# Down product of a gated FFN on one Trainium2 core: a Strassen recurrence with sums in SBUF, replaced by a plain product summed in PSUM over split operands that are prepared pair by pair

## Chip, cores and metric

One NeuronCore of a Trainium2 chip runs the whole kernel. The metric is the device time of one execution in microseconds (us); lower is better. TensorE (PE), VectorE (DVE), ScalarE (ACT), GpSimd (POOL) and the DMA queue of SyncE (SP) run side by side, each in its own instruction order, and wait for one another through semaphores.

## The reference

Two decoder layers over 1024 positions of width 1024, in float32. Layer 0 mixes with a recurrent mixer (RWKV-7), layer 1 with sparse attention (DSA); each mixer is followed by the same gated FFN. The change lies in the last lines of that FFN, in both layers:

```python
def conv_ffn(x, w_up, conv_w, conv_b, w_down):
    u = x @ w_up                                  # (1024, 1024) @ (1024, 5632)
    u = causal depthwise convolution of u, width 3, + conv_b
    gate, val = jnp.split(u, 2, axis=-1)
    return (jax.nn.silu(gate) * val) @ w_down     # (1024, 2816) @ (2816, 1024)
...
x = layer_norm(DN_ALPHA * x + f, ln_g[i, 1], ln_b[i, 1])
```

## The kernel before

`trunk` chains four phases: `rwkv`, `ffn` of layer 0, `dsa`, `ffn` of layer 1. Each is a generator, and `drive` lets a phase begin while the one ahead of it finishes: every `yield` of the phase ahead gives one turn to the next. A float32 product is made from two rounded parts: `split` (L54, L60) rounds an operand into a high part on ACT (L54) and subtracts it on POOL or DVE to get the low part (L60), and `mm3` (L65, L66, L67) issues three matmuls, high by high, high by low and low by high. What order the instructions of an engine stand in is decided when the program is built; within an engine nothing overtakes.

The FFN first makes the gated hidden rows and stores them to DRAM as eleven pairs of 128 rows, `hd[0]` to `hd[10]` (`gated`, L1039 to L1049). This part, the up product, is the same before and after. The down product then multiplies these 2816 rows with `w_down`.

Before, the down product is a Strassen-Winograd product: a pair p gives a 2 by 2 scheme of 512-wide blocks (two row blocks of the contraction; two halves of the positions, two halves of the columns), and seven products (`11`, `12`, `S1`, `S2`, `S3`, `S4`, `22`) take the place of eight. `d_load` reads a pair's hidden rows and weight rows, 1 MB each (L1135, L1136). `d_op` makes the sums and differences on DVE (`sub`, L908, and L1147) and splits the result (L54 on ACT, L60 on POOL or DVE). `down` runs the matmuls of one product for one block of 128 positions over the pairs of a group, into a PSUM bank (`dn`), and `add_to` adds that bank to the running sum `acc` in SBUF on DVE (L1166) before the next step may use the bank. Groups hold two or three pairs (`cuts`): ten pairs in layer 0, nine in layer 1. The blocks left over (`tail`: two in layer 0, four in layer 1) are multiplied plainly at the end (`dt`, L1260), row block by row block, each followed by the LayerNorm of these 128 positions and the store (`norm_store`, L149; the steps of the norm are L92 to L111).

In layer 0 this end is interleaved with the start of `dsa`, which loads `uq` and `uk`, multiplies them (`wqk`, L1326) in two groups with one load of `uk` each, splits and stores the results (L1334), loads and splits eight `win` tiles (L1339), then reads back the normed rows (`xr`, L1310), transposes them (`pt`, L1357) and starts the `win` product. All these DMAs go through SP's one queue, in order.

Of the kernel before, what the change touches and what calls it, by code (L numbers as in the profile page):

```python
# [7 lines left out]
F32 = mybir.dt.float32  # L8
F32R = mybir.dt.float32r
# [5 lines left out]
D = 1024  # L15
# [868 lines left out]
def ffn(k, layer, src, dst):  # L884
# [120 lines left out]
    def bank(name, pool=None):  # L1005
        return (pool or PX).tile([128, 512], F32, name=name, tag="b", bufs=4)
# [117 lines left out]
    NPAIR = NF // 2
    cuts = [0, 3, 6, 8, 10] if layer == 0 else [0, 3, 6, 9]
    groups = [range(a, b) for a, b in zip(cuts, cuts[1:])]
    in_P = (0, 3, 4, 8, 9) if layer == 0 else (0, 3, 6, 8)
    tail = range(2 * cuts[-1], NF)
    acc = []
    R = {}  # L1130

    def d_load(p):
        r = R[p] = dict(raw=big("raw", P_ if p in in_P else L_, (128, 8, 512), F32))
        raw = r["raw"]
        nc.sync.dma_start(raw[:, 0:4].rearrange("p (f a) c -> p f (a c)", f=2), hd[p].rearrange("f p c -> p f c"))  # L1135
        nc.sync.dma_start(  # L1136
            raw[:, 4:8].rearrange("p (f a) c -> p f (a c)", f=2),
            k.w_down[layer, p * 256 : (p + 1) * 256, :].rearrange("(f p) c -> p f c", p=128),
        )

    def d_op(p, n, pool, lo_eng):

        r = R[p]
        raw = r["raw"]
        if n == "S1":
            q = r["q"] = sm("q")
            nc.vector.tensor_tensor(q[:, 0], raw[:, 1], raw[:, 3], ALU.add)  # L1147
            sub(q[:, 1], raw[:, 5], raw[:, 4])
        elif n == "S2":
            q = r["q"]  # L1150
            sub(q[:, 0], q[:, 0], raw[:, 0])
            sub(q[:, 1], raw[:, 7], q[:, 1])
        elif n == "S3":
            sub(raw[:, 1:6:4], raw[:, 0:8:7], raw[:, 1:6:4])
        elif n == "S4":
            sub(raw[:, 2], raw[:, 2], r["q"][:, 0])
        elif n == "22":
            sub(raw[:, 6], raw[:, 6], r["q"][:, 1])
        hi, lo = t4("dh", F32R, pool, (128, 2, 512)), t4("dl", F32R, pool, (128, 2, 512))
        r[n] = hi, lo  # L1160
        at = {"11": slice(0, 5, 4), "12": slice(2, 7, 4), "S3": slice(1, 6, 4), "S4": slice(2, 8, 5), "22": slice(3, 7, 3)}
        split(k, raw[:, at[n]] if n in at else r["q"], hi, lo, "a", lo_eng)

    def add_to(hf, tt, ch, ps, first):
        o = acc[hf][:, tt, 512 * ch : 512 * ch + 512]
        nc.vector.scalar_tensor_tensor(o, o, ALPHA if first else 1.0, ps, ALU.mult, ALU.add)  # L1166

    B_ = {}

    def down(gi, n, tt):  # L1170
        new = n in ("11", "12", "S1")
        x = n in ("11", "S2", "S3", "22")
        if new:
            B_[x, tt] = bank("dn", PX if x else PY)
# [11 lines left out]
    for p in groups[0]:
        d_load(p)
    for hf in range(2):
        a = big("acc", L_, (128, 4, 1024), F32)
        acc.append(a)  # L1190
        for tt in range(4):
            nc.sync.dma_start(a[:, tt], src[(4 * hf + tt) * 128 : (4 * hf + tt + 1) * 128, :])
    ng = len(groups)
    dsteps = [(gi, n) for gi in range(ng) for n in ("11", "12", "S1", "S2", "S3", "S4", "22")]
    done = set()

    def d_ops(j):
        if j < len(dsteps) and j not in done:
            done.add(j)
            gi, n = dsteps[j]  # L1200
            for i, p in enumerate(groups[gi]):
                d_op(p, n, N_ if i == 2 else P_, CFG["dl0"][3 * j + i] if j < 3 else "v" if i == 2 and n in ("11", "12", "S4") else "p")

    hs = []

    def tail_op(f):

        if layer == 1 and f == NF - 1:
            room = [t4("to", F32R, N_) for _ in range(4)]
        else:  # L1210
            room = big("to", L_, (128, 4, 1024))
            room = [room[:, i] for i in range(4)]
        for i, ap in enumerate((hd[f // 2][f % 2], k.w_down[layer, f * 128 : (f + 1) * 128, :])):
            raw = t4("tr")
            nc.sync.dma_start(raw, ap)
            split(k, raw, room[2 * i], room[2 * i + 1], "a", "p")
        hs.append(room)

    late = [NF - CFG["gl"] + i for i in range(CFG["gl"])]
    for j, (gi, n) in enumerate(dsteps):  # L1220
        for x in CFG["ga"] if j == 0 else "":
            if x == "g":
                gated(late.pop(0))
            else:
                d_ops(int(x))
        d_ops(j)
        if n == "11" and gi + 1 < ng:
            for p in groups[gi + 1]:
                d_load(p)
        d_ops(j + 1)  # L1230
        if j == 0:
            while late:
                gated(late.pop(0))
        if gi == ng - 1 and n in ("S2", "S3", "S4") and (i := ("S2", "S3", "S4").index(n)) < len(tail):
            tail_op(tail[i])
        for tt in range(4):
            down(gi, n, tt)
    if len(tail) > 3:
        tail_op(tail[3])
    lnw = []  # L1240
    for z in range(2):
        if layer == 0:
            lnw.append(L_.tile([128, D], F32, name=f"lnw{z}"))
        else:
            lnw.append(sm("lnw").rearrange("p a b -> p (a b)"))
        i = B_LN + 4 * layer + 2 + z
        nc.sync.dma_start(lnw[z], k.bvec[i : i + 1, :].to_broadcast([128, D]))
# [3 lines left out]
    for tt in range(8):
        tsl = slice(128 * tt, 128 * tt + 128)
        r = [acc[tt // 4][:, tt % 4, 512 * ch : 512 * ch + 512] for ch in range(2)]
        sums = L_.tile([128, 2], F32, name="lns", tag="lns", bufs=2)
        for ch in range(2):
            cs = slice(512 * ch, 512 * ch + 512)
            ps = bank("dt")
            for i, (a, b, c, d) in enumerate(hs):
                mm3(k, ps, (a[:, tsl], b[:, tsl]), (c[:, cs], d[:, cs]), i == 0, i == len(hs) - 1)
            nc.vector.scalar_tensor_tensor(  # L1260
                r[ch], r[ch], 1.0, ps, ALU.mult, ALU.add, accum_out=sums[:, ch : ch + 1]
            )
        kw = {} if layer else dict(sums=sums, junk=L_.tile([128, 512], BF16, name="lnj", tag="lnj", bufs=1))
        norm_store(k, L_, r, lnw, dst, 128 * tt, CFG["ln4"][layer] if tt < 7 else "pv", **kw)
# [711 lines left out]
```

## Time and profile before

| what | value |
|---|---|
| time, median of 3 runs | 3173.01 us (3172.37 to 3178.31) |
| the profiled execution | 3170.01 us |
| its span in the profile | 3168.0 us |
| mean granted TensorE clock | 0.937 of full speed |
| PE busy | 2834.0 us (89%) |
| DVE busy | 2463.5 us (78%) |
| POOL busy | 1528.7 us (48%) |
| ACT busy | 1368.9 us (43%) |

The busy shares are means over four phases with different limits, so the stage in question is read by itself: a table of stages first (busy time of each engine and the granted clock in a stretch), then the waits ahead of the matmuls of that stretch, then the time line of the engine that is waited for. The granted clock is given as a share of 2.4 GHz; its two levels are 1.00 and 0.50.

### The profile page before, as it was taken

What the parts mean: (1) busy time and instruction counts of PE and PEld (TensorE: products, weight loads), DVE (VectorE), ACT (ScalarE), POOL (GpSimd) and SP (SyncE); (2) the same over time, 40 slices, a digit from 0 to 9 for tenths busy, and PEclk for the clock granted to TensorE, in tenths of its full rate; (3) what the DMA queues carried; (4) which work ended last, traced back from release to release, by engine and by line L of the source; (5) the groups of instructions that cost most, each with busy time, mean ns of one, the idle gap of its engine ahead of it and who ended that gap; (6) DMA issues with size and microseconds to landing.
All of it is one profiled execution on the core that took longest, in us unless ns stands there. A gap on an engine that the chain in (4) does not pass through costs nothing. (4 is left out here: it accounts for less than half of the span.)

```text
span 3168.0 us, 41686 instructions
## 1 busy us (share of the span) xinstructions
PE 2834.0 (89%) x15032; PEld 2217.4 (70%) x15032; DVE 2463.5 (78%) x3911; ACT 1368.9 (43%) x2353; POOL 1528.7 (48%) x987
## 2 busy tenths in 40 slices
PE   7789998898988999997888888889998899998798
PEld 3577576786866777775667765667776677777577
DVE  6776776768576888889786699995675888888965
ACT  4433243322233544443224487784363444444231
POOL 3525045140246666666677222212214666666766
PEclk9889998898998999998998989899999999999899
DMA  6645435344162222244115221113224222225212
GB/s 214 246 152 195 142 121 199 134 148 146 64 201 89 80 80 80 80 143 189 41 40 173 102 90 37 34 40 115 77 66 151 60 80 80 80 81 206 80 53 93
DMA packets 235232, 354.87 MB, mean 112 GB/s; under 512 B 17194, under 2 KB 110762, under 8 KB 234642
## 3 DMA queue, kind: packets, MB, share of 16 engines
q1 hardware_dynamic: 221202, 327.04, 31.6%
q10 hardware_dynamic: 13824, 25.17, 2.2%
q8 instruction: 118, 1.93, 0.3%
q14 instruction: 88, 0.72, 0.1%
HBM read 248.99 MB, written 103.15 MB: 111 GB/s over the span
## 5 line engine op out<-in xcount | busy, mean ns | idle before, releaser
L60 POOL TENSOR_TENSOR wo<-wr,wo 128x512 fp32r<-128x512 f32 x220 | 414.3, 1907 | 289.4 <-ACT wo L54 289.4
L1039 DVE SCALAR_TENSOR_TENSOR cv<-u,vec,cv 128x1023 f32<-128x1023 f32 (+1 forms) x176 | 348.0, 1995 | 52.9 <-ACT cv L1034 51.2
L65 PE MATMUL dn<-dh 128*128 128x512 f32 x532 | 220.3, 414 | 67.8 <-DVE acc L1166 67.8
L60 POOL TENSOR_TENSOR dl<-raw,dh 128x1024 fp32r<-128x1024 f32 x82 | 220.2, 2708 | 102.2 <-ACT dh L54 96.7
L65 PE MATMUL p<-xT,wo 128*128 128x512 f32 x528 | 213.1, 404 | 27.8 <-ACT u L1023 18.2
L66 PE MATMUL dn<-dl,dh 128*128 128x512 f32 x532 | 218.1, 410 | 14.3 <-DVE dl L60 7.5
L1671 POOL TENSOR_TENSOR cm<-sc,toep 128x256 f32<-128x256 f32 x96 | 75.7, 795 | 298.1 <-DVE mn L1687 229.7
L1034 ACT ACTIVATE cv<-u,vec 128x1024 f32<-128x1024 f32 x88 | 109.5, 1244 | 250.2 <-DVE u L1028 249.6
L67 PE MATMUL dn<-dh,dl 128*128 128x512 f32 x532 | 217.0, 408 | 0.0
L67 PE MATMUL p<-xT,wo 128*128 128x512 f32 x528 | 208.8, 395 | 2.9 <-POOL wo L60 2.9
L66 PE MATMUL p<-xT,wo 128*128 128x512 f32 x528 | 208.5, 395 | 3.0 <-DVE xT L60 3.0
L1166 DVE SCALAR_TENSOR_TENSOR acc<-acc,dn 128x512 f32<-128x512 f32 x196 | 131.0, 680 | 86.3 <-PE dn L67 86.3
L60 POOL TENSOR_TENSOR wo<-S,wo 128x512 fp32r<-128x512 f32 x88 | 173.3, 1987 | 30.0 <-ACT wo L54 25.7
L54 ACT CAST dh<-raw 128x1024 fp32r<-128x1024 f32 x95 | 94.8, 1047 | 199.6 <-issue 81.1
L65 PEld LDWEIGHTS dn<-dh 128*128 128x128 f32 x532 | 106.3, 200 | 98.5 <-DVE acc L1166 42.2
L60 POOL TENSOR_TENSOR wl<-wr,wh 128x512 fp32r<-128x512 f32 x56 | 76.3, 1363 | 181.7 <-ACT wh L54 109.1
L65 PEld LDWEIGHTS p<-xT,wo 128*128 128x128 f32 x528 | 100.7, 191 | 65.4 <-ACT u L1023 33.0
L65 PE MATMUL p<-x,wo 128*128 128x512 f32 x352 | 138.9, 394 | 3.4 <-DVE x L60 3.0
L54 ACT CAST wo<-wr 128x512 fp32r<-128x512 f32 x220 | 127.2, 619 | 27.3 <-POOL wo L60 18.6
L67 PE MATMUL p<-x,wo 128*128 128x512 f32 x352 | 138.4, 393 | 0.0
L66 PE MATMUL p<-x,wo 128*128 128x512 f32 x352 | 138.4, 393 | 0.0
L66 PEld LDWEIGHTS dn<-dl,dh 128*128 128x128 f32 x532 | 106.5, 200 | 38.4 <-DVE dl L60 8.4
(412 smaller groups left out, 8552.0 us busy)
## 6 DMA issues: line engine op xcount, KB each, us to landing
wr<-in_w_up_dram SPq DMA_DIRECT2D x88, 512.0 KB, 5.9
hd<-cv SPq DMA_DIRECT2D x44, 512.0 KB, 3.4
raw<-hd SPq DMA_DIRECT2D x19, 1024.0 KB, 5.0
raw<-in_w_down_dram SPq DMA_DIRECT2D x19, 1024.0 KB, 7.6
wr<-in_w_wo_dram SPq DMA_DIRECT2D x68, 256.0 KB, 2.9
wr<-in_w_rkv_dram SPq DMA_DIRECT2D x48, 256.0 KB, 4.3
kept_w<-wh ACTq DMA_DIRECT2D x48, 256.0 KB, 3.5
kept_w<-wl SPq DMA_DIRECT2D x48, 256.0 KB, 3.0
```

Source lines behind the costliest of these rows:

```text
L54: nc.scalar.copy(hi, raw)
L60: eng.tensor_tensor(lo, raw, f32(hi), ALU.subtract)
L65: mm(ps, lhs[0], rhs[0], start=start, stop=False, **kw)
L66: mm(ps, lhs[0], rhs[1], start=False, stop=False, **kw)
L67: mm(ps, lhs[1], rhs[0], start=False, stop=stop, **kw)
L1034: nc.scalar.activation(o, u, AF.Identity, bias=k.vec[:, cb : cb + 1], scale=k.vec[:, cw[2] : cw[2] + 1])
L1039: nc.vector.scalar_tensor_tensor(o[:, d:], u[:, : 1024 - d], k.vec[:, cw[j] : cw[j] + 1], o[:, d:], ALU.mult, ALU.add)
L1166: nc.vector.scalar_tensor_tensor(o, o, ALPHA if first else 1.0, ps, ALU.mult, ALU.add)
L1671: (nc.vector if CFG["cm"][h4] == "v" else nc.gpsimd).tensor_tensor(cm[:, :near], mk, toep[g][:, h % 8, 256 - near :], ALU.add)
```

## The change

The Strassen scheme, its sums on DVE and its running sum in SBUF go. The product is plain: the positions are taken in two halves (`hf`), and for each half eight PSUM banks, four blocks of 128 positions by two halves of the columns, hold their sums over all eleven pairs. `d_prep` makes a pair ready two steps ahead: it loads 512 positions of the pair's hidden rows (`hr`) and the pair's two weight rows of 1024 columns (`dr`), splits them into `hh`, `hl` and `wd`. `wd` lies in a buffer of 16 KB per partition: in layer 0 in one of three (pool `P_`), in layer 1 by turns in `P_` (two) and `L_` (five). Each pair's weights are loaded and split once for each half. The last two pairs of a half (`LAST`) are done bank by bank in `d_end`, which then adds the residual and leaves the finished row (one DVE instruction, L1167); `d_norm` norms a block when both its banks are done. In layer 0 the four second-column banks of the second half are finished before the pools are closed and `dsa` may start.

```diff
-    def d_op(p, n, pool, lo_eng):
...
-            sub(q[:, 0], q[:, 0], raw[:, 0])
-            sub(q[:, 1], raw[:, 7], q[:, 1])
...
-    def add_to(hf, tt, ch, ps, first):
-        o = acc[hf][:, tt, 512 * ch : 512 * ch + 512]
-        nc.vector.scalar_tensor_tensor(o, o, ALPHA if first else 1.0, ps, ALU.mult, ALU.add)
...
-    def down(gi, n, tt):
...
-        add_to(hf, tt, ch, ps, gi == 0 and n in ("11", "S1", "S2", "22"))
...
+    NPAIR, LAST = NF // 2, 2
...
+    def d_prep(hf, p):
+        late = hf == 1 and p >= NPAIR - LAST
+        hr = t4("hr")
+        nc.sync.dma_start(
+            hr.rearrange("p (f c) -> p f c", f=2), hd[p][:, :, 512 * hf : 512 * hf + 512].rearrange("f p c -> p f c")
+        )
...
+        w = big("wd", L_ if late or layer and (hf * NPAIR + p) % 2 else P_, (128, 4, 1024))
+        split(k, hr, *h, "a", "p" if layer and hf and p < 4 else "v")
+        for f in range(2):
+            wr = t4("dr", pool=N_)
+            nc.sync.dma_start(wr, k.w_down[layer, (2 * p + f) * 128 : (2 * p + f + 1) * 128, :])
+            split(k, wr, w[:, 2 * f], w[:, 2 * f + 1], "a", "p")
+        ops[hf, p] = *h, w
+
+    def d_mm(ps, hf, p, tt, ch):
+        hh, hl, w = ops[hf, p]
+        for f in range(2):
...
+            mm3(
+                k, ps, (hh[:, ts], hl[:, ts]), (w[:, 2 * f, cs], w[:, 2 * f + 1, cs]), p == f == 0,
+                p == NPAIR - 1 and f == 1,
+            )
+
+    def d_end(ps, hf, tt, ch):
+        for p in range(NPAIR - LAST, NPAIR):
+            d_mm(ps, hf, p, tt, ch)
...
+        r = rows[hf][:, tt, 512 * ch : 512 * ch + 512]
+        nc.vector.scalar_tensor_tensor(
+            r, r, ALPHA, ps, ALU.mult, ALU.add, accum_out=sums[hf, tt][:, ch : ch + 1]
+        )
...
+    for s in steps[:2]:
+        d_prep(*s)
+    for f in range(NF - CFG["gl"], NF):
+        gated(f)
+    order = [(ch, tt) for ch in (1, 0) for tt in range(4)]
+    for i, (hf, p) in enumerate(steps):
+        if i + 2 < len(steps):
+            d_prep(*steps[i + 2])
...
+        if p < NPAIR - LAST:
+            for ch, tt in order:
+                d_mm(bk[ch, tt], hf, p, tt, ch)
...
+        if (hf, p) == (0, NPAIR - 1):
+            for ch, tt in order:
+                d_end(bk[ch, tt], 0, tt, ch)
+                if ch == 0:
+                    d_norm(0, tt)
+    for tt in range(4):
+        d_end(bk[1, tt], 1, tt, 1)
     if layer == 0:
         pools.close(P_, N_, PY)
         yield
...
+    for tt in range(4):
+        d_end(bk[0, tt], 1, tt, 0)
+        d_norm(1, tt)
         if layer == 0:
             yield
```

The first place is DVE in the down product of layer 0. Before, soon after its first matmuls (`acc<-acc,dn` adds a bank to the running sum, the `L908` and `L1147` rows are the sums and differences of the scheme):

```order
L1166 SCALAR_TENSOR_TENSOR acc<-acc,dn 128x512
L908 TENSOR_TENSOR raw<-raw,q 128x512 x3
L1166 SCALAR_TENSOR_TENSOR acc<-acc,dn 128x512
L908 TENSOR_TENSOR raw<-raw,q 128x512 x2
L1166 SCALAR_TENSOR_TENSOR acc<-acc,dn 128x512
L1147 TENSOR_TENSOR q<-raw 128x512
L908 TENSOR_TENSOR q<-raw 128x512
L1166 SCALAR_TENSOR_TENSOR acc<-acc,dn 128x512
```

With the change, DVE's rows from the end of the up product to the first finished blocks of the first half (`hl<-hr,hh` is the low part of a pair's hidden rows, L98 to L108 are the norm of a block):

```order
L60 TENSOR_TENSOR hl<-hr,hh 128x1024 x11
L1167 SCALAR_TENSOR_TENSOR acc,lns<-acc,dn 128x512 x5
L98 TENSOR_SCALAR lnm<-lns 128x1
L99 TENSOR_SCALAR lno<-lnm 128x1
L106 SCALAR_TENSOR_TENSOR acc<-acc,lnm,lnw_11890 128x512
L1167 SCALAR_TENSOR_TENSOR acc,lns<-acc,dn 128x512
L102 TENSOR_SCALAR lnve<-lnv 128x1
L98 TENSOR_SCALAR lnm<-lns 128x1
L104 SCALAR_TENSOR_TENSOR lnnm<-lnm,lnrs 128x1
L108 SCALAR_TENSOR_TENSOR acc<-acc,lnrs,lnw_11892 128x512
L99 TENSOR_SCALAR lno<-lnm 128x1
L106 SCALAR_TENSOR_TENSOR acc<-acc,lnm,lnw_11890 128x512
```

The adds of banks and the scheme's sums between them are gone; DVE has eleven low parts in a row with no add between, and the adds that remain stand among the norms at the end of a half.

The second place is SP's queue where layer 0 ends and `dsa` begins (`uk`, `wr<-in_w_in` are loads, `wqk` are stores, `x<-acc` stores of normed rows, `xr<-x` their reading back). Before, from the first load for `win`:

```order
L1339 DMA wr<-in_w_in_dram 128x456 x3
L1334 DMA wqk<-wqkh 128x512
L1334 DMA wqk<-wqkl 128x512
L1339 DMA wr<-in_w_in_dram 128x456
L1334 DMA wqk<-wqkh 128x512
L1334 DMA wqk<-wqkl 128x512
L1339 DMA wr<-in_w_in_dram 128x456
...
L1319 DMA uk<-in_w_uk_dram 128x512
L1339 DMA wr<-in_w_in_dram 128x456
L149 DMA x_0_74<-acc 128x512
L1339 DMA wr<-in_w_in_dram 128x456
L149 DMA x_0_74<-acc 128x512
```

With the change, the same place:

```order
L1294 DMA wr<-in_w_in_dram 128x456 x8
L1289 DMA wqk<-wqkh 128x512
L1289 DMA wqk<-wqkl 128x512
...
L1274 DMA uk<-in_w_uk_dram 128x512
L149 DMA x_4_78<-acc 128x512 x2
L149 DMA x_5_79<-acc 128x512
L1289 DMA wqk<-wqkh 128x512
...
L1298 DMA grow<-in_dsa_rows_dram 128x512
L1265 DMA xr<-x_0_74 128x512 x2
```

All eight loads for `win` now stand ahead of the first store of `wqk`, the stores of rows 0 to 3 are far earlier, and the first reading back still stands behind the last store of `wqk`.

## Rows read from the trace of the kernel before

**Rows 1.** Table of stages: length, busy us (instructions) by engine, PEclk, DMA share, GB/s.
```profile
1300.00:1437.80 137.80, 133.80 (x584) 108.86 (x583) 116.61 (x85) 63.95 (x95) 94.97 (x49) 1.00 0.44 139
1437.80:1692.70 254.90, 208.01 (x841) 166.16 (x840) 201.09 (x186) 73.60 (x74) 173.24 (x66) 0.90 0.20 75
1692.70:1738.80 46.10, 36.75 (x177) 29.97 (x176) 35.25 (x80) 29.17 (x61) 35.63 (x30) 0.86 0.68 226
2893.00:3115.00 222.00, 186.82 (x758) 150.44 (x757) 174.16 (x154) 70.23 (x71) 157.34 (x60) 0.90 0.23 86
```
**Rows 2.** Time line of PE, layer 0: start, length, instruction, idle before and releaser.
```profile
1437.82 0.39 PE L65 MATMUL dn<-dh 128*128 128x512 f32 x1
...
1447.34 0.39 PE L65 MATMUL dn<-dh 128*128 128x512 f32 x1
...
1497.84 0.79 PE L65 MATMUL dn<-dh 128*128 128x512 f32 x1 [13.24 <-DVE acc L1166]
```
**Rows 3.** Groups by line on PE, 1437.8 to 1692.7: busy, mean ns, idle before.
```profile
L65 PE MATMUL dn<-dh 128*128 128x512 f32 x280 | 115.5, 413 | 38.2 <-DVE acc L1166 38.2
L66 PE MATMUL dn<-dl,dh 128*128 128x512 f32 x280 | 114.8, 410 | 8.7 <-DVE dl L60 4.6 <-POOL dl L60 4.1
```
**Rows 4.** The same view, 2893 to 3115 (layer 1).
```profile
L65 PE MATMUL dn<-dh 128*128 128x512 f32 x252 | 104.8, 416 | 29.6 <-DVE acc L1166 29.6
L66 PE MATMUL dn<-dl,dh 128*128 128x512 f32 x252 | 103.2, 410 | 5.6 <-DVE dl L60 2.9 <-POOL dl L60 2.7
```
**Rows 5.** Time line of DVE, 1465 to 1500, around the longest wait of layer 0.
```profile
1466.39 0.68 DVE L908 TENSOR_TENSOR q<-q,raw 128x512 f32<-128x512 f32 x1
...
1471.61 7.81 DVE L908 TENSOR_TENSOR raw<-raw,q 128x512 f32<-128x512 f32 x3
...
1495.97 1.21 DVE L60 TENSOR_TENSOR dl<-raw,dh 128x1024 fp32r<-128x1024 f32 x1
```
**Rows 6.** The page's costliest groups: busy, mean ns of one, idle before.
```profile
L60 POOL TENSOR_TENSOR dl<-raw,dh 128x1024 fp32r<-128x1024 f32 x82 | 220.2, 2708 | 102.2 <-ACT dh L54 96.7
L1166 DVE SCALAR_TENSOR_TENSOR acc<-acc,dn 128x512 f32<-128x512 f32 x196 | 131.0, 680 | 86.3 <-PE dn L67 86.3
L54 ACT CAST dh<-raw 128x1024 fp32r<-128x1024 f32 x95 | 94.8, 1047 | 199.6 <-issue 81.1
```
**Rows 7.** DMA issues, 1437.8 to 1692.7: count, KB each, median us to landing.
```profile
tr<-in_w_down_dram SPq DMA_DIRECT2D x2, 512.0 KB, 4.4
```
**Rows 8.** Time line of PE where layer 0 ends and `dsa` begins.
```profile
1695.52 3.50 PE L1326 MATMUL wqk<-uk,uq 64*128 64x128 f32 x32
1713.86 5.24 PE L1326 MATMUL wqk<-uk,uq 64*128 64x128 f32 x32 [3.62 <-DMA uk<-in_w_uk_dram]
1733.00 1.94 PE L1357 MATMUL pt<-ident,xr 128*128 128x128 f32 x8 [3.42 <-DMA xr<-x]
1738.80 0.73 PE L65 MATMUL win<-win,X 128*128 128x456 f32 x1
```
**Rows 9.** Time line of SP's queue at the same place.
```profile
1710.16 0.42 SPq L1319 DMA_DIRECT2D uk<-in_w_uk_dram  x1
1730.16 2.81 SPq L1310 DMA_DIRECT2D xr<-x  x6
```
**Rows 10.** Time lines of PE, POOL, ACT and DVE in layer 1: first `dn`, last rows.
```profile
2893.11 0.39 PE L65 MATMUL dn<-dh 128*128 128x512 f32 x1
...
3158.51 0.39 PE L67 MATMUL dt<-to 128*128 128x512 f32 x1
...
3158.91 1.27 POOL L111 TENSOR_TENSOR acc<-acc,lnw 128x512 f32<-128x512 f32 x1
3160.87 0.99 POOL L103 TENSOR_TENSOR lnrs<-lnve,mhalf 128x1 f32<-128x1 f32 x1 [0.69 <-DVE lnve L95]
3162.97 1.26 POOL L110 TENSOR_TENSOR acc<-acc,lnw 128x512 f32<-128x512 f32 x1 [1.12 <-ACT acc L107]
...
3162.08 0.81 ACT L107 ACTIVATE acc<-acc,lnnm,lnrs 128x512 f32<-128x512 f32 x1 [4.62 <-DVE lnnm L104]
...
3164.27 0.69 DVE L111 TENSOR_TENSOR acc<-acc,lnw 128x512 f32<-128x512 f32 x1 [1.56 <-POOL acc L110]
```

More of the change, by code (lines that the diff above doesn't have):

```diff
@@ L1121, in ffn @@
             gated(f)
[L1124 to L1135, printed above, removed]
+    NPAIR, LAST = NF // 2, 2
@@ L1136, in d_load @@
+    ops, hold, lnw, sums, rows = {}, {}, [], {}, {}
+    def d_prep(hf, p):
+        late = hf == 1 and p >= NPAIR - LAST
+        hr = t4("hr")
         nc.sync.dma_start(
-            raw[:, 4:8].rearrange("p (f a) c -> p f (a c)", f=2),
-            k.w_down[layer, p * 256 : (p + 1) * 256, :].rearrange("(f p) c -> p f c", p=128),
-        )
-    def d_op(p, n, pool, lo_eng):
[L1143 to L1150, printed above, removed]
-            sub(q[:, 0], q[:, 0], raw[:, 0])
-            sub(q[:, 1], raw[:, 7], q[:, 1])
[L1153 to L1162, printed above, removed]
@@ L1186, in ffn @@
[L1186 to L1202, printed above, removed]
@@ L1204, in ffn @@
[L1204 to L1247, printed above, removed]
+            hr.rearrange("p (f c) -> p f c", f=2), hd[p][:, :, 512 * hf : 512 * hf + 512].rearrange("f p c -> p f c")
+        )
@@ new lines, in d_prep @@
+        if late:
+            if not hold:
+                hold["h"] = big("hl", L_, (128, 4, 1024))
+            i = 2 * (p - NPAIR + LAST)
+            h = hold["h"][:, i], hold["h"][:, i + 1]
+        else:
+            h = t4("hh", F32R), t4("hl", F32R)
+        w = big("wd", L_ if late or layer and (hf * NPAIR + p) % 2 else P_, (128, 4, 1024))
[4 more added lines that the diff above has]
+            split(k, wr, w[:, 2 * f], w[:, 2 * f + 1], "a", "p")
@@ new lines, in d_norm @@
+    def d_norm(hf, tt):
+        r = [rows[hf][:, tt, 512 * ch : 512 * ch + 512] for ch in range(2)]
+        kw = {} if layer else dict(
+            sums=sums[hf, tt], junk=L_.tile([128, 512], BF16, name="lnj", tag="lnj", bufs=1)
+        )
+        norm_store(
+            k, L_, r, lnw, dst, 128 * (4 * hf + tt), CFG["ln4"][layer] if (hf, tt) != (1, 3) else "pv", **kw
+        )
+    steps = [(hf, p) for hf in range(2) for p in range(NPAIR)]
+    for s in steps[:2]:
+        d_prep(*s)
+    for f in range(NF - CFG["gl"], NF):
+        gated(f)
@@ new lines, in ffn @@
+    order = [(ch, tt) for ch in (1, 0) for tt in range(4)]
+    for i, (hf, p) in enumerate(steps):
+        if i + 2 < len(steps):
+            d_prep(*steps[i + 2])
+        if p == 0:
+            bk = {x: bank("dn", PX if x[0] == 0 else PY) for x in order}
+        if p < NPAIR - LAST:
+            for ch, tt in order:
+                d_mm(bk[ch, tt], hf, p, tt, ch)
+        if p == 4:
+            rows[hf] = big("acc", L_, (128, 4, 1024), F32)
+            for tt in range(4):
+                nc.sync.dma_start(rows[hf][:, tt], src[(4 * hf + tt) * 128 : (4 * hf + tt + 1) * 128, :])
+            for z in range(0 if lnw else 2):
+                if layer == 0:
+                    lnw.append(L_.tile([128, D], F32, name=f"lnw{z}"))
+                else:
+                    lnw.append(sm("lnw").rearrange("p a b -> p (a b)"))
+                i_ = B_LN + 4 * layer + 2 + z
+                nc.sync.dma_start(lnw[z], k.bvec[i_ : i_ + 1, :].to_broadcast([128, D]))
+        if (hf, p) == (0, NPAIR - 1):
[3 more added lines that the diff above has]
+                    d_norm(0, tt)
@@ L1250, in ffn @@
         yield
[L1251 to L1264, printed above, removed]
+        for tt in range(4):
+            yield
+    for tt in range(4):
+        d_end(bk[0, tt], 1, tt, 0)
+        d_norm(1, tt)
         if layer == 0:
```

16 lines of the change are left out of this document (4 added, 12 removed).

## The prediction

> **What bounds the kernel now.** I read the table of stages first, then the waits ahead of PE's matmuls, then DVE's time line where those waits end.
>
> In the table [rows 1] the up product runs PE at 133.80 of 137.80 us with a granted clock of 1.00. The down product of layer 0 (1437.8 to 1692.7) has PE at 208.01 of 254.90 us and a clock of 0.90, with DVE at 201.09; layer 1's has 186.82 of 222.00, also 0.90. So PE waits inside the down product, and pays a second time in the clock.
>
> How much: 43 matmul rows start between 1437.82 and 1447.34 [rows 2], so a matmul costs 9.52 / 42 = 0.2267 us at the full clock. Layer 0's stage holds 840 of them, 190.4 us, and lasts 254.9: 64.5 us are lost. Layer 1's holds 756, 171.4 us, and lasts 222.0: 50.6 are lost. The wait groups name the first part of it: 38.2 + 8.7 us in layer 0 [rows 3] and 29.6 + 5.6 in layer 1 [rows 4], nearly all "until DVE acc L1166", the add that frees a PSUM bank. The remaining 33 us are the lower clock after the waits and small gaps.
>
> Why the add is late stands in DVE's time line [rows 5]: three of the scheme's subtractions take 7.81 us in front of an add, 2.6 each, where one alone takes 0.68. DVE bounds this stage, with its own arithmetic and with adds queued behind it.
>
> **The change, part by part, against the profiled execution (3170.0 us; the median of the runs shown is 3.0 higher).**
>
> *Matmuls.* Plain: 2 halves x 11 pairs x 2 rows x 8 banks x 3 = 1056 per layer, where before there were 840 + 96 and 756 + 192. That adds 120 and 108, together 228 x 0.2267 = 51.7 us of PE. This is the price; it lies on the path.
>
> *DVE.* 196 adds of 0.680 us [rows 6] and all L908 and L1147 work go. In their place come 32 adds and 44 low parts (some on POOL in layer 1) of about 1.2 us [rows 5]. A step of 48 matmuls takes 10.9 us, so DVE is off the path inside a half.
>
> *Preparation.* A step needs 2 weight splits on POOL (2 x 2.71 us), 3 casts on ACT (3 x 1.05) [rows 6] and 1.5 MB of loads, 512 KB landing in 4.4 us [rows 7]. POOL is the fullest at 5.4 of 10.9 us, so I cost the second loading and splitting of the weights at nothing. Its cover is PE's step and a lead of two steps; without the cover it is the rival that ends slower. The hidden rows and weights of the first pairs don't depend on the last two gated rows, and the buffers of the first two pairs come free before the up product ends, so I take no wait at the start.
>
> *Layer 0 to `dsa`.* The product starts where it did (1437.8) and its matmuls end 239.4 us later, at 1677.2. `dsa` starts its `wqk` product after 1012 of them, at 1667.2. Before, from the first `wqk` matmul (1695.52) to the issue of the second `uk` load took 14.6 us, and from there to the first `win` matmul (1738.80) 28.6 [rows 8, 9]. If the whole chain keeps its length, `win` starts at 1710.5: a gain of 28.3. If it vanishes under PE's work, `win` starts after the last matmul, two `wqk` groups (2 x 3.50) and 16 transposes (3.9) [rows 8], at 1688.1: a gain of 50.7. I take 10 us for the first leg, because the win loads that stood between the `wqk` stores in SP's queue are now ahead of them, and keep the second, where the reading back of x still stands behind the last `wqk` store and norms share POOL: 1705.8, a gain of 33.0. That is nearer to the low end, since the queue's order keeps the chain.
>
> *Layer 1 to the end.* From 2893.1 [rows 10] the matmuls end at 3132.5, where before the last one ended at 3158.7: 26.2 us gained. The end behind it grows. Blocks now finish every 12 matmuls, 2.72 us. A block's norm passes POOL, ACT, POOL, POOL in order: 0.99 + 0.81 + 1.26 + 1.27 [rows 10] and some 0.35 of passing on, 4.7 us. Three such periods are 14.1 against 8.2 of PE, so the last block comes 6 us later behind the last matmul than before. Bounds: 0 if the norms overlap, 10 if POOL and DVE hinder each other. Gain 20.
>
> *The end of the first half.* New: all eight banks are finished in 21.8 us, and the second half needs them back. The last bank is wanted 8.2 us (three more blocks) + 5.4 (four banks of the other column half) + 4.1 (three banks) = 17.7 us after the first column-0 bank is done. Its add stands on DVE behind two blocks' norms, 2 x 4.7 = 9.4 us, and seven instructions with two SBUF inputs, including a low part. What such an instruction pays beside a busy POOL is 2.6 less 0.68, some 1.9 us at most [rows 5]. Bounds: 9.4, no wait, and 9.4 + 13.4 + a split of 2.7 = 25.5, a wait of 8 and a restart at half clock, some 10. I take 4 per layer, as POOL has norm steps of 1.3 rather than splits of 2.7 for most of that stretch in layer 0.
>
> The row shows the slow subtractions beside POOL's splits. The Trainium skill ("SBUF — State Buffer", section "SBUF: two separate sides") has a rule that would explain it and speaks against this change: a VectorE instruction with two SBUF inputs and a GpSimd instruction that reads SBUF exclude each other for the whole instruction, the later one blocking. By that rule, the trace of before agrees with 2.6 against 0.68 us; taken in full, a whole split ahead of each of the seven, it is the third case below.
>
> Sum: 33.0 + 20 - 8 = 45 us gained, 3125 on the profiled execution; with a part of its 3.0 us to the median, **3126**.
>
> **Rivals.**
>
> *Better: everything hides.* The join goes at PE's pace (50.7) and the half's end and the last norms cost little (20 to 26, no waits): a gain of 71 to 77, 3093 to 3099, some 3098 for the median. For it: rows 0 to 3 are normed long before they are read. Against: SP's order, above. Chance 0.12.
>
> *Weaker: norm and split block each other at both half ends.* Each of DVE's seven two-input instructions waits for a whole POOL split, 7 x 2.7 = 19 us: 28.4 against 17.7, a wait of 11 per layer in place of 4, and the last norms at their upper bound: 45 - 14 - 4 = 27, so 3143 to 3145. For it: 2.6 us in rows 5. Against: POOL is not full there. Chance 0.17.
>
> *Slower: preparation becomes the bound.* If a pair's chain does not run two steps ahead, because a big buffer or a `dr` buffer comes free only when the pair before last is multiplied, a step lasts load + cast and split twice + hidden rows: 4.4 + 1.05 + 2 x 2.71 + 1.05 + 1.2 = 13.1 us against 10.9, 2.2 x 44 = 97 us more: 3170 - 45 + 97 = 3222. It decides from (45 / 44) = 1.0 us per step on, that is at 11.9 us. Against it: layer 0 has three big buffers and layer 1 seven, six or more for `dr`, and the before-stage moved 75 GB/s where this needs 1.5 MB in 10.9 us, 138, as the up product's last stretch does (139) [rows 1]. Chance 0.08, with everything near it; a milder form, a wait of some 0.5 us per step, ends at 3147 (0.03).
>
> *That the change doesn't do what it says* is out for the sums: DVE's order shows eleven low parts with no add between them.
>
> **How the numbers follow.** Forecast (3108 to 3140) 0.60, better 0.12, weaker 0.17, mild starvation 0.03, slower or no gain 0.08. A measurement of this kernel can tell about 0.2%, 6.3 us. No change needs 3167 to 3179, which only a partly starved step gives: 0.02. Slower 0.06. Faster 0.92. The range 3097 to 3150 holds the forecast, the weaker case and most of the better one, and leaves out some 0.15.
>
> **What would show it.** Right: in both down stages a granted clock near 1.00 and 1056 matmuls in 240 to 250 us; no wait on DVE's add except at the end of the first half, under 5 us; the first `win` matmul near 1706; last matmul to end of span some 15 us where it was 9. Wrong: waits on `wd` or `hl` in every step (preparation), a clock of 0.90 again, `win` after 1715, or a wait at each half's end above 10 us.

## The result and the profile after

The changed kernel takes 3131.77 us (median of 4 runs, 3125.03 to 3143.64), the kernel before, timed with it, 3175.66 us (4 runs, 3172.37 to 3185.30). The ratio is 0.9861, with a 95% interval of 0.9822 to 0.9899: 44 us faster, where 3126 us was forecast. The profiled execution took 3143.64 us, span 3141.8, mean granted TensorE clock 0.940.

Table of stages of the changed kernel, cut at the first `dn` of layer 0, 239.4 us after it, at the first `win`, the first `dn` of layer 1 and the end of its last matmul; columns as in [rows 1]. In layer 0 the 239.4 us hold the first `wqk` group, and some 15 of the product's 1056 matmuls come behind them, the last at 1713.25.

```profile
0.00:1465.80 1465.80, 1335.66 (x8089) 1031.83 (x8090) 1073.79 (x1362) 557.56 (x901) 645.33 (x444) 0.91 0.42 136
1465.80:1705.20 239.40, 239.40 (x1074) 198.42 (x1073) 79.34 (x86) 86.18 (x107) 128.43 (x62) 1.00 0.49 170
1705.20:1733.70 28.50, 10.74 (x66) 9.34 (x64) 12.09 (x30) 13.44 (x27) 17.38 (x16) 0.73 0.60 213
1733.70:2886.40 1152.70, 1047.72 (x4982) 822.90 (x4981) 909.97 (x2020) 627.72 (x1232) 476.10 (x359) 0.96 0.26 79
2886.40:3125.80 239.40, 239.40 (x1057) 198.08 (x1055) 83.12 (x96) 70.86 (x72) 133.29 (x60) 1.00 0.44 160
3125.80:3141.80 16.00, 0.13 (x1) 0.00 (x0) 7.64 (x18) 2.44 (x3) 8.71 (x8) 0.57 0.31 115
```

In both products PE is now busy for the whole of these 239 us at a clock of 1.00, and DVE for a third of it, where PE waited and the clock stood at 0.90 before [rows 1]. No gap between two matmuls of either product is longer than 0.4 us, apart from the two in which `wqk` runs. The groups that took the place of [rows 6]: POOL's splits of the weights, DVE's of the hidden rows, and the matmuls that are the first to use a pair's high and low parts.

```profile
L60 POOL TENSOR_TENSOR wd<-dr,wd 128x1024 fp32r<-128x1024 f32 x88 | 224.6, 2574 | 134.4 <-ACT wd L54 126.0
L65 PE MATMUL dn<-wd,hh 128*128 128x512 f32 x640 | 249.0, 389 | 0.0
L66 PE MATMUL dn<-wd,hh 128*128 128x512 f32 x640 | 249.0, 389 | 0.0
L60 DVE TENSOR_TENSOR hl<-hr,hh 128x1024 fp32r<-128x1024 f32 x36 | 61.8, 1716 | 155.2 <-ACT hh L54 86.0
```

So the matmuls wait for nothing that is prepared for them: the idle time ahead of them is 0.0. Against the first profile of the kernel before, the table gives three differences. From the first `dn` of layer 0 to the first `win`: 1438 to 1739 before, 301.0 us, now 267.9, a gain of 33.1. From the first `dn` of layer 1 to the end of the span: 274.9 before, now 255.4, a gain of 19.5. And the first `dn` itself starts at 1465.8 where it stood at 1437.8, 28.0 us later, in a part of the program that the change does not touch. The last one eats over half of the first two in this pair of profiles. It is taken up by six executions below.

Layer 0's end as [rows 8, 9] showed it, first on PE, then in SP's queue.

```profile
1695.23 3.50 PE L1281 MATMUL wqk<-uk,uq 64*128 64x128 f32 x32
...
1707.69 3.47 PE L1281 MATMUL wqk<-uk,uq 64*128 64x128 f32 x32 [1.01 <-DMA uk<-in_w_uk_dram]
...
1730.39 3.65 PE L1312 MATMUL pt<-ident,xr 128*128 128x128 f32 x16 [16.75 <-DMA xr<-x]
1733.69 0.73 PE L65 MATMUL win<-win,X 128*128 128x456 f32 x1
```
```profile
1704.78 0.39 SPq L1274 DMA_DIRECT2D uk<-in_w_uk_dram  x1
...
1724.57 0.32 SPq L1289 DMA_DIRECT2D wqk<-wqkl  x1
...
1725.44 8.95 SPq L1265 DMA_DIRECT2D xr<-x  x10
```

The longest wait that is left here is PE's 16.75 us for `xr`. That load is issued at 1725.44, behind the last store of `wqk` in SP's queue.

The end of the first half in layer 0, on DVE: the first column-0 bank is added at 1577.47, the last at 1592.58.

```profile
1577.47 0.69 DVE L1167 SCALAR_TENSOR_TENSOR acc<-acc,dn 128x512 f32<-128x512 f32 x1 [2.02 <-PE dn L67]
...
1581.68 0.16 DVE L104 SCALAR_TENSOR_TENSOR lnnm<-lnm,lnrs 128x1 f32<-128x1 f32 x1 [0.54 <-POOL lnrs L103]
1581.76 0.74 DVE L108 SCALAR_TENSOR_TENSOR acc<-acc,lnrs,lnw 128x512 f32<-128x512 f32 x1
...
1587.36 2.35 DVE L104 SCALAR_TENSOR_TENSOR lnnm<-lnm,lnrs 128x1 f32<-128x1 f32 x1 [0.44 <-POOL lnrs L103]
1589.63 2.96 DVE L108 SCALAR_TENSOR_TENSOR acc<-acc,lnrs,lnw 128x512 f32<-128x512 f32 x1
...
1592.58 0.67 DVE L1167 SCALAR_TENSOR_TENSOR acc<-acc,dn 128x512 f32<-128x512 f32 x1
```

The same two instructions of the norm (L104, L108) take 0.16 and 0.74 us for one block, and 2.35 and 2.96 for the next. Beside the second pair POOL runs two weight splits, here on its time line:

```profile
1587.30 4.75 POOL L60 TENSOR_TENSOR wd<-dr,wd 128x1024 fp32r<-128x1024 f32 x2
```

The last rows, on POOL: the first step of each block's norm (L103).

```profile
3120.20 0.99 POOL L103 TENSOR_TENSOR lnrs<-lnve,mhalf 128x1 f32<-128x1 f32 x1 [31.83 <-DVE lnve L95]
...
3125.14 1.00 POOL L103 TENSOR_TENSOR lnrs<-lnve,mhalf 128x1 f32<-128x1 f32 x1
...
3130.34 0.54 POOL L103 TENSOR_TENSOR lnrs<-lnve,mhalf 128x1 f32<-128x1 f32 x1
...
3135.10 0.55 POOL L103 TENSOR_TENSOR lnrs<-lnve,mhalf 128x1 f32<-128x1 f32 x1
```

The norms start every 4.8 to 5.2 us, while PE finishes a block every 2.72. The span ends 16.3 us after the start of the last matmul, where it was 9.5 before.

### The profile page after: what moved, and what is told of

It reads as the page before. It is cut to its first block, busy times and chain, and to the rows that moved or that the text cites. A ratio compares the mean times of both kernels' runs of the same rounds, so it can differ in the third digit from the quotient of the medians.

```text
span 3141.8 us, 41842 instructions
## 1 busy us (share of the span) xinstructions
PE 2873.0 (91%) x15260; PEld 2260.6 (72%) x15260; DVE 2165.9 (69%) x3609; ACT 1358.2 (43%) x2340; POOL 1409.2 (45%) x947
## 5 line engine op out<-in xcount | busy, mean ns | idle before, releaser
L60 POOL TENSOR_TENSOR wd<-dr,wd 128x1024 fp32r<-128x1024 f32 x88 | 224.6, 2574 | 134.4 <-ACT wd L54 126.0
L67 PE MATMUL dn<-wd,hl 128*128 128x512 f32 x704 | 274.0, 389 | 0.0
L65 PE MATMUL dn<-wd,hh 128*128 128x512 f32 x640 | 249.0, 389 | 0.0
L66 PE MATMUL dn<-wd,hh 128*128 128x512 f32 x640 | 249.0, 389 | 0.0
L60 DVE TENSOR_TENSOR hl<-hr,hh 128x1024 fp32r<-128x1024 f32 x36 | 61.8, 1716 | 155.2 <-ACT hh L54 86.0
L67 PEld LDWEIGHTS dn<-wd,hl 128*128 128x128 f32 x704 | 132.2, 188 | 27.5
L54 ACT CAST wd<-dr 128x1024 fp32r<-128x1024 f32 x88 | 89.5, 1050 | 113.5 <-DMA dr<-in_w_down_dram 49.3
L66 PEld LDWEIGHTS dn<-wd,hh 128*128 128x128 f32 x640 | 120.1, 188 | 25.1
L65 PEld LDWEIGHTS dn<-wd,hh 128*128 128x128 f32 x640 | 120.1, 188 | 24.7
```

## The experiments

Each profiled execution is read by the same marks: when the first `dn` starts, how long it is from there to the first `win`, and from layer 1's first `dn` to the end of the span.

| kernel | execution, us | first `dn` at | `dn` to `win`, layer 0 | `dn` to end, layer 1 |
|---|---|---|---|---|
| before | 3170.01 | 1437.8 | 301.0 | 274.9 |
| before, repeated | 3178.59 | 1445.6 | 301.8 | 273.6 |
| before, third | 3170.37 | 1441.9 | 300.3 | 274.9 |
| before, fourth | 3187.49 | 1458.4 | 300.3 | 273.7 |
| changed | 3143.64 | 1465.8 | 267.9 | 255.4 |
| changed, repeated | 3131.92 | 1454.0 | 268.1 | 255.4 |
| changed, third | 3123.89 | 1446.1 | 269.5 | 255.4 |
| changed, fourth | 3130.68 | 1452.5 | 268.6 | 255.4 |
| rows read early | 3117.38 | 1453.5 | 254.6 | 255.4 |
| last banks row by row | 3124.28 | 1453.5 | 268.9 | 248.7 |
| both of these | 3103.99 | 1450.3 | 254.2 | 248.6 |
| Strassen without sums | 3075.45 | 1446.0 | 243.3 | 232.4 |
| plain, summed in SBUF | 3167.37 | 1458.5 | 282.8 | 272.3 |
| one pool in layer 1 | 3148.84 | 1452.6 | 268.0 | 272.1 |

### Both kernels again: is the late start of the product theirs?

Nothing is edited. On every engine and in SP's queue both kernels have the same instructions in the same order until some 29 us ahead of the first `dn`, where the preparation of the first pairs begins to differ.

> The changed kernel once more. Theory A: everything ahead of the first down-product matmul is the same program, so its length differs between executions by chance, through TensorE's clock in the recurrent mixer; here it again lies anywhere from 1430 to 1470 us, while the stages the change touches repeat: first dn to first win matmul 267 to 270 us, first dn of layer 1 to the end 254 to 257 us. Rival B: the change makes the first part slower by its mere presence: again 1460 us or more, and the gain stays near 44 us for that reason.

> The kernel before once more, for a second profile. Theory A: its part ahead of the first down-product matmul differs from the first profile's 1437.8 us by some 5 to 30 us by chance, and its two down stages repeat within 3 us (301 and 275 us). Rival B: it repeats 1438 within 3 us, so that the 1465.8 of the changed kernel has a cause in the change.

> The kernel before, once more, for the start of layer 0's first dn matmul alone. So far: 1437.8, 1445.6 and 1446.0 (this kernel twice, and the one without the sums, which has its down product) against 1450.3 to 1465.8 in seven executions of the changed kernel and its variants, whose program up to that point is the same. Theory A (the part ahead varies by itself, the same way for both): this one falls anywhere from 1437 to 1466, and two and two of them mix. Theory B (the changed program starts its down product some 12 us later, for a cause outside its instructions): 1437 to 1448. The stage down product to win 300 to 303 and layer 1's to the end 273 to 276 under both.

> The changed kernel, once more, for the same number. Theory A: anywhere from 1437 to 1466. Theory B: 1450 to 1466. Its stages 267 to 269 and 255 to 256 under both.

> The kernel before, a fourth time. Theory A: the first dn anywhere from 1437 to 1466. Theory B: 1437 to 1448.

> The changed kernel, a fourth time. Theory A: the first dn anywhere from 1437 to 1466. Theory B: 1450 to 1466.

The stages repeat: 300.3 to 301.8 and 273.6 to 274.9 us in four executions before, 267.9 to 269.5 and 255.4 in four after. The start of the first `dn` doesn't: 1437.8 to 1458.4 before, 1446.1 to 1465.8 after. The part up to there is cut here at the first transpose of the FFN (`pt`, L932), behind which the up product follows: before (its first execution), changed (its first), and the first piece of before in its fourth execution.

```profile
0.00:941.30 941.30, 835.13 (x6050) 626.24 (x6050) 672.24 (x1024) 333.94 (x560) 316.56 (x264) 0.91 0.48 162
941.30:1437.80 496.50, 470.57 (x2040) 380.27 (x2040) 411.03 (x345) 223.93 (x343) 333.97 (x181) 0.98 0.34 103
```
```profile
0.00:970.00 970.00, 863.62 (x6049) 650.83 (x6050) 671.15 (x1024) 334.12 (x560) 316.41 (x264) 0.88 0.47 157
970.00:1465.80 495.80, 472.03 (x2041) 381.00 (x2041) 402.63 (x339) 223.43 (x342) 328.93 (x180) 0.98 0.32 95
```
```profile
0.00:962.30 962.30, 860.52 (x6050) 647.52 (x6051) 672.91 (x1024) 334.31 (x560) 316.43 (x264) 0.88 0.47 158
```

In the first piece PE does the same 6049 or 6050 matmuls and is busy for 835.13, 863.62 and 860.52 us, while DVE, ACT and POOL stay within 2 us. The granted clock goes with it, 0.91, 0.88 and 0.88. So that piece is longer by about the time for which PE was granted the lower clock. It moves the start by 21 us between executions of one program.

The spread is complete at this transpose. It stands at 941.3 to 962.3 us in the four executions before and at 949.6 to 970.0 in the four after, and from there to the first `dn` it is 495.4 to 497.1 us in all eight. That is over 460 us ahead of the first instruction in which the programs differ, so none of the changed instructions makes the start late.

Theory B, a constant shift of some 12 us by the changed program, misses both its bounds: the fourth execution of before starts at 1458.4, above 1448, and the third of the changed kernel at 1446.1, below 1450. Theory A holds as far as four and four can tell. The means are 1445.9 and 1454.6; over all rows of the table, whose programs are the same but for those last 29 us, 1445.9 (five that begin the Strassen product) and 1454.1 (nine that begin the plain one). The third and fourth executions of both kernels, run one after another, have means of 1450 and 1449. So a tendency of a few us, by a cause outside the instructions, is neither shown nor excluded. The stages' 32.3 and 18.9 us, less these 8.7 and with 1.3 from the stretch between the stages, make the difference of the mean spans: 3174.6 against 3130.7, 44 us.

In another set of timing runs the changed kernel had 3126.74 us (3121.37 to 3131.92) against 3180.38, a ratio of 0.9823 (0.9796 to 0.9850), 54 to 56 us. One set gave 44, the other near to what the stages hold.

### The rows of x read early: where does layer 0's join stand?

In `dsa`, four loads of rows 0 to 3 go into one buffer ahead of `uq`, instead of behind the `wqk` stores.

```diff
+    xe = P_.tile([128, 4, 1024], F32, name="xe", tag="big", bufs=3)
+    for tt in range(4):
+        nc.sync.dma_start(xe[:, tt], src[tt * 128 : tt * 128 + 128, :])
     def x_load(tt):
         rows[tt] = []
+        if tt < 4:
+            rows[tt] = [xe[:, tt, 512 * g : 512 * g + 512] for g in range(2)]
+            return
```

> Rows 0 to 3 of the next phase's input are loaded into a buffer of their own, ahead of all other loads of that phase. Theory: the 16.75 us in which PE waits for the reading back of x come only from its place behind the last wqk store; with it gone the first win matmul starts some 15 us earlier (first dn to first win 252 us in place of 268) and the time falls by 12 to 17 us. Rival: the win product needs later work of the same stretch too (win splits, the rows 4 to 7 that are normed last), so that PE waits a little later instead and less than 5 us remain.

Measured: 3112.78 us median, ratio to before 0.9792 (0.9765 to 0.9819), against the changed kernel's 0.9823 in the same set of runs: 14.0 us less. The stage is 254.6 us, 13.5 less. PE's time line there:

```profile
1696.52 3.47 PE L1288 MATMUL wqk<-uk,uq 64*128 64x128 f32 x32 [1.24 <-DMA uk<-in_w_uk_dram]
...
1701.16 0.66 PE L1319 MATMUL pt<-ident,xe 128*128 128x128 f32 x4 [1.17 <-ACT wqk L1292]
1703.10 1.12 PE L1319 MATMUL pt<-ident,xe 128*128 128x128 f32 x4 [1.29 <-ACT wqk L1292]
...
1708.05 0.44 PE L65 MATMUL win<-win,X 128*128 128x456 f32 x1 [0.61 <-DVE X L1325]
```

The 16.75 us wait for `xr` is gone, and waits of 1.3 us and less stand in its place. What ended the stage was in the prediction's second leg: the reading back behind the last `wqk` store.

### Layer 1's last banks row by row: what makes the end longer?

The last eight banks are finished in the order of the rows instead of column by column, so that the two banks of a row end together and rows come 24 matmuls apart.

```diff
-    for tt in range(4):
+    for tt in range(4 if layer == 0 else 0):
         d_end(bk[1, tt], 1, tt, 1)
...
     for tt in range(4):
+        if layer:
+            d_end(bk[1, tt], 1, tt, 1)
         d_end(bk[0, tt], 1, tt, 0)
         d_norm(1, tt)
```

> In layer 1 the last eight banks are finished block by block (both column halves of a block, then its norm) and not column half by column half. Theory: the last norms are late because blocks finish every 2.72 us and a norm needs 4.7 us through POOL and ACT; with a block every 5.44 us the end behind the last matmul is 9 to 10 us in place of 16, and the time falls by 6 to 7. Rival: the norm's own chain is slower now for another reason (its rows in another buffer, DVE beside POOL): no change.

Measured: 3119.55 us, ratio to before 0.9808 (0.9784 to 0.9833), 7.2 us under the changed kernel. The time from the last matmul to the end is back at 9.6 us, and the L103 steps are 5.4 us apart, with POOL idle ahead of each:

```profile
3112.90:3122.50 9.60, 0.46 (x3) 0.04 (x1) 4.09 (x10) 0.81 (x1) 3.92 (x4) 0.66 0.27 99
```
```profile
3109.89 0.99 POOL L103 TENSOR_TENSOR lnrs<-lnve,mhalf 128x1 f32<-128x1 f32 x1 [0.68 <-DVE lnve L95]
...
3115.34 0.99 POOL L103 TENSOR_TENSOR lnrs<-lnve,mhalf 128x1 f32<-128x1 f32 x1 [0.69 <-DVE lnve L95]
```

POOL now waits for the block (0.68 us for DVE), not the block for POOL. The longer end of the changed kernel is the queue of norms on POOL behind blocks that come every 2.72 us.

### Both edits in one kernel

> Both of the edits above together. Theory: they lie in different layers and add up: 18 to 24 us faster than the changed kernel, some 3105 to 3112 us where that one takes 3130. Rival: only one of them pays.

Measured: 3102.35 us (3099.48 to 3113.11), ratio to before 0.9756 (0.9730 to 0.9781). That is 24.4 us under the changed kernel in the same set of runs, with 14.0 and 7.2 for the parts. The stages add up exactly (254.2 and 248.6 us), so some 3 of the 24.4 come from elsewhere, within the scatter of the first part. This version is faster than both kernels.

### The Strassen product without its sums: what held the kernel before?

In the kernel before, the sums and differences of blocks are left out, and the seven products multiply blocks as they are. Loads, splits, matmuls and adds stay.

```diff
-        if n == "S1":
-            q = r["q"] = sm("q")
-            nc.vector.tensor_tensor(q[:, 0], raw[:, 1], raw[:, 3], ALU.add)
-            sub(q[:, 1], raw[:, 5], raw[:, 4])
...
-            sub(raw[:, 6], raw[:, 6], r["q"][:, 1])
```

> The kernel before without the Strassen sums and differences on DVE in the down product (the L908 and L1147 work; the products are taken of unsummed blocks, so that part of the computation is left out). Theory: these sums, standing ahead of the adds that free PSUM banks, are what PE waits for: the waits on DVE fall from 47 us (layer 0) and 35 (layer 1) to under 10 each, the clock goes to about 1.00 and the time falls by 80 to 110 us against the kernel before. Rival: the adds into SBUF by themselves, with every bank waiting for its add, hold PE: at least half of the waits stay and the time falls by less than 50.

Measured: 3083.61 us, ratio to before 0.9685 (0.9661 to 0.9709), 103 us less than the 3186.49 of the kernel before, timed with it. Its two stages, 1446.0 being the first `dn` of layer 0:

```profile
1446.00:1689.30 243.30, 231.29 (x1018) 189.79 (x1016) 135.88 (x204) 100.90 (x134) 199.45 (x95) 0.96 0.33 121
2841.20:3064.20 223.00, 216.86 (x949) 178.73 (x947) 126.69 (x180) 75.58 (x78) 172.68 (x80) 0.99 0.26 96
```

The same adds into SBUF are still there, but the waits that the trace of before put down to them, 38.2 and 29.6 us [rows 3, 4], are nearly gone: 0 in layer 0, where 4.4 us for low parts are left, and 4.2 in layer 1. First layer 0, then layer 1:

```profile
L65 PE MATMUL dn<-dh 128*128 128x512 f32 x280 | 109.4, 391 | 0.0
```
```profile
L65 PE MATMUL dn<-dh 128*128 128x512 f32 x252 | 98.8, 392 | 4.2 <-DVE acc L1152 4.2
```

So it was the sums on DVE, queued ahead of the adds, that held PE. How much of this is the number of sums, and how much that one takes 2.6 us in place of 0.68 where POOL splits [rows 5], the runs do not separate. This kernel also bounds what the 228 added matmuls cost: the plain product's stages are 268.5 (mean of four) and 255.4 us against 243.3 and 232.4, 25 + 23 = 48 us, where the prediction charged 51.7. These 48 us are not the matmuls alone: in layer 1 the plain product has an end that is 6.8 us longer, and the kernel without sums loses 8 us to waits and a lower clock (its 948 matmuls at 0.2267 us are 214.9 of 223.0 us).

### The plain product summed in SBUF: does PSUM summing matter by itself?

The changed kernel, but each pair's bank is added to the running sum on DVE, as before, instead of being summed in PSUM over all eleven pairs; only the last two are summed there. The rows that the sum starts from are loaded at a half's first step for that, not at its fifth.

```diff
             mm3(
-                k, ps, (hh[:, ts], hl[:, ts]), (w[:, 2 * f, cs], w[:, 2 * f + 1, cs]), p == f == 0,
-                p == NPAIR - 1 and f == 1,
+                k, ps, (hh[:, ts], hl[:, ts]), (w[:, 2 * f, cs], w[:, 2 * f + 1, cs]), f == 0 and p <= NPAIR - LAST, f == 1 and p != NPAIR - LAST,
             )
...
                 d_mm(bk[ch, tt], hf, p, tt, ch)
+                r = rows[hf][:, tt, 512 * ch : 512 * ch + 512]
+                nc.vector.scalar_tensor_tensor(r, r, 1.0 if p else ALPHA, bk[ch, tt], ALU.mult, ALU.add)
```

> The changed kernel with one part undone: each pair's product is added to a running sum in SBUF by DVE (288 adds of 0.68 us more), only the last two pairs are summed in PSUM. Theory: where the sums are kept does not matter as long as DVE has room; 8 adds take 5.5 of a step's 10.9 us and a bank has 9.5 us until it is wanted, so PE still runs without waits and the time is within 6 us of the changed kernel's. Rival: the sums in PSUM are what pays: adds beside POOL's splits come late, PE waits in every step and the time rises by more than 20 us.

My theory fell. Measured: 3156.83 us, ratio to before 0.9922 (0.9892 to 0.9952). The stages grew by 14.3 and 16.9 us over the means of four, 31.2 together, where within 6 was expected. The rival had the size right and the place wrong: the waits are not in every step. In layer 0 there are two of them, 11.4 us in all. The groups by line on PE, then the longer wait on PE, then DVE at that place:

```profile
L65 PE MATMUL dn<-wd,hh 128*128 128x512 f32 x320 | 126.0, 394 | 11.4 <-DVE acc L1197 11.4
```
```profile
1479.36 0.79 PE L65 MATMUL dn<-wd,hh 128*128 128x512 f32 x1 [8.48 <-DVE acc L1197]
```
```profile
1464.61 0.68 DVE L1197 SCALAR_TENSOR_TENSOR acc<-acc,dn 128x512 f32<-128x512 f32 x1
1465.21 2.47 DVE L1039 SCALAR_TENSOR_TENSOR cv<-u,vec,cv 128x1022 f32<-128x1022 f32 x2
...
1468.73 3.42 DVE L1039 SCALAR_TENSOR_TENSOR cv<-u,vec,cv 128x1022 f32<-128x1022 f32 x1
1472.07 3.36 DVE L60 TENSOR_TENSOR hl<-hr,hh 128x1024 fp32r<-128x1024 f32 x1
1475.35 3.36 DVE L1048 TENSOR_TENSOR cv<-cv 128x1024 f32<-128x1024 f32 x1
1478.63 2.46 DVE L1197 SCALAR_TENSOR_TENSOR acc<-acc,dn 128x512 f32<-128x512 f32 x4
```

Between two adds DVE still works through the convolution of the last gated rows and a low part. That takes 13 us, and PE has by then used up its banks. The other waits stand at the starts of halves too: in layer 1's first half behind the same work (6.25 us), in both second halves behind the norms of the first half or a low part (1.3 to 2.9 us each). DVE was not full in this stage (184.0 of 282.8 us); what counts is how late it is where a half begins. Sums that stay in PSUM for a half ask nothing of DVE there.

### One pool for the weights of layer 1

The weights of all pairs but the last two go into the one pool, in layer 1 with a lead of one step instead of two.

```diff
-        w = big("wd", L_ if late or layer and (hf * NPAIR + p) % 2 else P_, (128, 4, 1024))
+        w = big("wd", L_ if late else P_, (128, 4, 1024))
...
-    for s in steps[:2]:
+    lead = 1 if layer else 2
+    for s in steps[:lead]:
         d_prep(*s)
```

> The changed kernel with the alternation undone in layer 1: all weight rows but the last two pairs' of the second half go through the one pool with two buffers, prepared one step ahead in place of two. Theory: inside a half a step's split work (6 us) fits into one step, so PE waits only where both buffers are held to the end of the first half and the next pair is split after it: one wait of 5 to 8 us in layer 1 and a few us of lower clock, 6 to 12 us in all. Rival C: there is slack everywhere: no change. Rival D: with one step of lead PE waits in every step: more than 30 us.

Measured: 3149.98 us, ratio to before 0.9909 (0.9880 to 0.9937). Layer 1's stage is 16.7 us longer, where 6 to 12 were expected; layer 0's is unchanged (268.0). PE now waits for splits, 9.2 us in all, most around the end of the first half, and the granted clock is 0.82 there (2980 to 3012). The two longest waits on PE, then POOL and ACT at the second of them:

```profile
2979.79 0.79 PE L66 MATMUL dn<-wd,hh 128*128 128x512 f32 x1 [2.33 <-POOL wd L60]
...
3007.83 0.79 PE L66 MATMUL dn<-wd,hh 128*128 128x512 f32 x1 [3.90 <-POOL wd L60]
```
```profile
2997.21 0.99 POOL L103 TENSOR_TENSOR lnrs<-lnve,mhalf 128x1 f32<-128x1 f32 x1 [15.15 <-DVE lnve L95]
...
3003.11 2.35 POOL L60 TENSOR_TENSOR hl<-hr,hh 128x1024 fp32r<-128x1024 f32 x1
3005.42 5.12 POOL L60 TENSOR_TENSOR wd<-dr,wd 128x1024 fp32r<-128x1024 f32 x2
```
```profile
3001.62 2.00 ACT L54 CAST wd<-dr 128x1024 fp32r<-128x1024 f32 x2 [2.37 <-PE dn L67]
```

POOL stands idle for 15.15 us first. The casts of the pair's weights begin on ACT only at 3001.62, released by a matmul of the product: the buffers are held to the end of the first half, as the theory said. POOL then has a norm step and a low part of hidden rows ahead of the weights' split.

With the two buffers of a single pool the preparation runs one step ahead, and a step's slack is not enough there. The two-pool rotation of the change buys the second step. The edit takes away the second pool and the second step together; a single pool with the full lead, which would need a third buffer of 16 KB per partition in it, was not tried.

## Why the prediction was right

*What bound the kernel before: DVE, with its own arithmetic and with adds queued behind it.* Shown by the kernel without sums: with the same adds, the waits for DVE's add go from 38.2 to 0 us and from 29.6 to 4.2. The prediction's "nearly all" is too strong: of the 82.1 us that its wait groups name, 14.3 are for low parts, and without the sums 6.4 of these are left.

*Matmuls, +51.7 us.* 1056 matmuls in 239.4 us without a gap in layer 1 are 0.2267 us each, the figure that the price was worked out with. The stages cost 48 us more than those of a Strassen product that is hardly held up, which fits: some 8 us of waits on that side and 6.8 of longer end on this one nearly cancel.

*Preparation costs nothing.* Right: no wait in either product. The low parts on DVE took 1.72 us for the 1.2 charged, which cost nothing, as DVE was busy for a third of the stage. The cover that was named, a lead of two steps, is needed in layer 1: with one step and one pool 16.7 us are lost. The slower rival, preparation as the bound, has its mechanism in that kernel, at a sixth of its price: the waits stand at a few places, not in each of 44 steps.

*Layer 0 to `dsa`, 33.0 us.* Right in total, 33.1 in the first pair and 32.3 in the means of four, and by its two legs. From the first `wqk` matmul (1695.23) to the issue of the second `uk` load (1704.78) it is 9.6 us for the 10 taken; from there to `win` (1733.69) 28.9 for 28.6. That 14 us of the second leg come from the queue's order is shown by the early rows. The prediction's sign of being wrong, `win` after 1715, came true by the letter in all four executions (1715.6 to 1733.7): it was given as a time from the program's start, and the start of the product moved. The better rival's claim that the join could go at PE's pace holds for the edited kernel, not for the change.

*Layer 1 to the end, 20 us.* 19.5 in the first pair, 18.9 in the means. The end grew by 6.8 us where 6 was worked out, by the mechanism named: three periods of the norm chain take 14.9 us (3120.20 to 3135.10) for 14.1.

*The end of the first half, 4 us per layer: the step that was mis-sized.* Measured 0 in both layers. The add of the last bank was allowed 17.7 us behind the first column-0 bank, and came after 15.1 (13.7 in layer 1), so the lower bound of that term held. DVE met POOL's splits once in each layer, with two instructions that in layer 0 together took 5.3 us for 0.9; seven such meetings were the upper bound. POOL has weight splits for 4.75 of the 15.1 us and is idle or in the norms for the rest, as the prediction said when it took a value near the low end. That the slow sums of before stood beside POOL's splits, which [rows 5] do not show, is in the trace of before; POOL at that place:

```profile
1473.29 2.78 POOL L60 TENSOR_TENSOR dl<-q,dh 128x1024 fp32r<-128x1024 f32 x1
```

The rule of the Trainium skill ("SBUF — State Buffer", section "SBUF: two separate sides") is that a VectorE instruction with two SBUF inputs and a GpSimd instruction that reads SBUF exclude each other. The trace agrees: the same instruction on one element per partition takes 2.35 us beside a split and 0.16 without. Whether the weaker rival would come true with a fuller POOL, as that rule would have it, no run here shows.

*The sum, 45 us.* The stages give 32.3 + 18.9 = 51 in the means of four and 53 in the first pair, for 45: the missing 6 to 8 are the term for the first half's end. The time came out at 3131.77, not near 3120. In the traces the part ahead of the product is longer in the changed kernel, by 28.0 us in the first pair and by 8.7 in the means; of the other timing runs there is no trace, so for the median this cause is inferred. The sentence "the product starts where it did (1437.8)" had no term for that: it starts anywhere from 1437.8 to 1465.8. Of the two errors, +8 and about -9, neither was seen, and they nearly cancel: that the forecast of 3126 came so near is luck to that extent. In the other set of runs, with a ratio of 0.9823, they did not. The profiled execution of 3143.64 us lies where the weaker rival was put (3143 to 3145), but has none of its waits; the late start alone puts it there.

## What to carry to other kernels

A wait that a trace puts down to a short instruction, here the 0.68 us add, may belong to what stands ahead of it on its engine. Take the queue away, not the instruction, and see whether the wait goes. Fewer matmuls are worth less than the time their operands cost on an engine that PE waits for: seven products with their sums in DVE's queue lost to eight without, though the same seven without sums, which compute something else, take 48 us less than the eight. When a bound is lifted, look at the next two places in the same trace, here a read queued behind stores and a chain of norms behind bunched blocks; they gave another 24 us for a few lines each.

## What the runs showed of the hardware

The granted clock of a long stretch that is not changed varies between executions: in two executions of the kernel before it was 0.91 and 0.88 in layer 0's mixer, the first 941 and 962 us, while the up product behind it took 495.4 to 497.1 us in all eight. Those 21 us are half of what this change gives, and far more than the 0.2% that a median was taken to tell. The start of the stage in question must be compared before a gain is read from two spans.

In the plain product, a granted clock of 1.00 was kept for 239 us in a row in both layers, at 0.2267 us per matmul of the product, with 170 GB/s of DMA beside it in layer 0.

An instruction on a single element per partition (L104) took 2.35 us beside a split on POOL of 2.4 us, where it takes 0.16 alone: here the smallest step paid as much as a large one, a 128x512 step (L108) taking 2.96 for 0.74.
